# Pairs of channels parted by ScalarE ahead of the matmuls, in a matmul with a decayed cumulative sum

## The chip, the cores and the metric

The kernel runs on one core of a Trainium2 chip. The metric is device time in microseconds (us); three runs of the kernel before gave 987.27, 988.52 and 989.05 us, median 988.52. The engines are PE (TensorE, with its weight loads listed as PEld), DVE (VectorE), ACT (ScalarE), POOL (GpSimd) and SP (SyncE, which here only issues DMAs). Each works through its own queue in order.

## The reference

```python
B, S, D = 16, 2048, 1024                      # x is B x S x D, w is D x D, decay is D
xw = x @ w
out[:, 0, :] = xw[:, 0, :]
for t in range(1, S):
    out[:, t, :] = decay[None, :] * out[:, t - 1, :] + xw[:, t, :]
```

A matmul over channels, and then along time, for each batch and output channel, a first-order recurrence. Everything is float32 outside; the matmul runs in bf16.

## The kernel before

**Chunks and groups.** Time is cut into 64 chunks of 512 steps (four to a batch). A group is one or two chunks; the output of a group is made in eight tiles n = 0 to 7 of 128 output channels, T = 512 or 1024 time steps wide. The groups are [0], [1], then pairs [2, 3] to [60, 61], then [62] and [63] (L126). The word slot is used for one tile's turn in the order of the program, and step for its number over the whole run in the changed kernel.

**Input.** `load(c, q)` (L107) is a DMA from POOL's queue that brings a quarter of the channels of chunk c, turned to bf16 on the way, into 32 partitions of a buffer `xb` (four buffers). `turn(c)` (L117) transposes a whole chunk on DVE in blocks of 32 x 32. It treats two neighbouring bf16 channels as one float32, so that one transpose of 2048 float32 does for the chunk; in the result `xt` the two channels of a pair lie side by side at every time step, `[128, M, TL, 2]`. The matmul for channel block k reads `xt[:, k // 2, :, k % 2]`, every second bf16 (L136).

**Matmul.** Each tile takes eight matmuls of 128 x 128 by 128 x 512 per chunk (k = 0 to 7), accumulated in PSUM. Three PSUM buffers of T = 1024 rotate. In the first group the first six tiles are computed with k outermost, while the weights still arrive (`heads`, L277 on). 4096 matmuls in all.

**The recurrence.** A plain tile is scanned by DVE straight out of PSUM over all T steps (L193), which also frees the PSUM buffer. A tile whose n is in `PAIRED` (five of the eight) goes another way. `pair()` (L168): ACT copies the tile out of PSUM into `xs` (L172) and makes decay times the even steps (L162); POOL adds that to the odd steps (L178). `scan()`: DVE scans only the odd steps, with decay squared (`dec2`), T/2 long (L184). `complete()`: ACT multiplies the odd results by decay (L162 again) and POOL adds the even inputs (L206); ACT also keeps the last step for the next group (L209). `back()` (L211) transposes a finished tile on DVE into the output buffer `ot` (two buffers, which also hold the raw weights at the start). After tile 7 of a group `store` sends `ot` out in four DMAs, one per quarter of the partitions, on SP's queue. The last group has no pairwise tiles, and stores in two halves.

**What sets the order.** `pin` keeps instructions in the order of the program on their engines. `behind(new)` writes that order: `pair` of the new tile, the scan of the tile before it if pairwise, the scan of the new tile if plain, `complete` of the tile before, and then `back`: of a pairwise tile two slots after its matmuls, of a plain one a slot after. `feed(step, after)` (L243) follows each tile: at n = 1 and n = 4 it turns the chunks of the next group and appends the loads that their buffers then allow; then it issues one load, or two if more than four wait.

**The start.** Loads of chunk 0, 16 loads of the weights, eight weight copies (DVE and ACT in turn, L98 and L100) and four tiny loads of decay on ACT's queue behind ACT's copies; then the loads of chunks 1 to 3 and, on DVE, the product `dec2` (L85) and `turn(0)`.

Of the kernel before, what the change touches and what calls it, by code (L numbers as in the profile page):

```python
# [9 lines left out]
FP32 = mybir.dt.float32  # L10
BF16 = mybir.dt.bfloat16
ALU = mybir.AluOpType


def _ap(ap_obj: bass.AP, new_ap, extra_offset=0):
    return dataclasses.replace(
        ap_obj,
        ap=[list(p) for p in new_ap],
        offset=ap_obj.offset + extra_offset,
    )  # L20
# [5 lines left out]
def kernel(  # L26
# [17 lines left out]

    nc = tc.nc
    pin = tc.keep_in_program_order
    B, S, D = x.shape  # L50
# [2 lines left out]
    NQ = 4  # L53
    P = 32
    CQ = D // NQ
    K = CQ // P
    M = K // 2
    TL = 512
    NJ = TL // P
    NC = S // TL  # L60
    PAIRED = (0, 1, 3, 4, 6)
    TURNS = (1, 4)

    const = ctx.enter_context(tc.tile_pool(name="const", bufs=1))
    xbp = ctx.enter_context(tc.tile_pool(name="xbp", bufs=4))
    xtp = ctx.enter_context(tc.tile_pool(name="xtp", bufs=4))
    sop = ctx.enter_context(tc.tile_pool(name="sop", bufs=4))
    tmp = ctx.enter_context(tc.tile_pool(name="tmp", bufs=2))
    otp = ctx.enter_context(tc.tile_pool(name="otp", bufs=2))
    psp = ctx.enter_context(tc.tile_pool(name="psp", bufs=3, space=bass.MemoryType.PSUM))  # L70
    pdp = ctx.enter_context(tc.tile_pool(name="pdp", bufs=1, space=bass.MemoryType.PSUM))

    def quad(q):
        return slice(q * P, (q + 1) * P)

    dec = const.tile([128, K], FP32, name="dec")
    dec2 = pdp.tile([128, 512], FP32, name="dec2")
    wsb = const.tile([128, K, K, NQ, P], BF16, name="wsb")

    def load_dec():  # L80
        with nc.allow_non_contiguous_dma(reason="a vector of 1024"):
            for q in range(NQ):
                pin(nc.scalar.dma_start(
                    out=dec[quad(q), :], in_=_ap(decay, [[1, P], [P, K]], q * CQ)))
        pin(nc.vector.tensor_tensor(out=dec2[:, 0:K], in0=dec, in1=dec, op=ALU.mult))  # L85

    def load_w():
        wb = otp.tile([128, M, 2 * D], BF16, name="ot")
        for m in range(M):
            for q in range(NQ):  # L90
                pin(nc.gpsimd.dma_start(  # L91
                    out=wb[quad(q), m],
                    in_=_ap(w, [[2 * D, P], [1, 2 * D]], (q * CQ + m * 2 * P) * D)))
        for k in range(K):
            dst = wsb[:, k].rearrange("p n q i -> p q n i")
            src = wb.rearrange("p m (e q n i) -> p (m e) q n i", e=2, q=NQ, n=K)[:, k]
            if k % 2:
                pin(nc.scalar.copy(out=dst, in_=src))  # L98
            else:
                pin(nc.vector.tensor_copy(out=dst, in_=src))  # L100

    chunks = [(b, c * TL) for b in range(B) for c in range(NC)]
    nch = len(chunks)
    xt_of = {}
    xb_of = {}

    def load(c, q):  # L107
        if c >= nch:
            return
        b, t0 = chunks[c]  # L110
        if q == 0:
            xb_of[c] = xbp.tile([128, NJ, CQ], BF16, name="xb")
        pin(nc.gpsimd.dma_start(  # L113
            out=xb_of[c][quad(q)],
            in_=_ap(x, [[D, P], [P * D, NJ], [1, CQ]], (b * S + t0) * D + q * CQ)))

    def turn(c):  # L117
        xt = xtp.tile([128, M, TL, 2], BF16, name="xt")
        src = xb_of.pop(c).rearrange("p j c -> p (j c)").bitcast(FP32)
        dst = xt.rearrange("p m t e -> p (m t e)").bitcast(FP32)  # L120
        pin(nc.vector.transpose(  # L121
            out=dst.rearrange("p (m j i) -> p j m i", m=M, i=P),
            in_=src.rearrange("p (j m c) -> p j m c", m=M, c=P)))
        xt_of[c] = xt

    groups = [[0], [1]] + [[c, c + 1] for c in range(2, nch - 2, 2)] + [[nch - 2], [nch - 1]]  # L126
    for g in groups:
        assert chunks[g[0]][0] == chunks[g[-1]][0]

# [2 lines left out]
    def matmul(ps, n, k, xt):  # L132
        pin(nc.tensor.matmul(  # L133
            out=ps,
            lhsT=wsb[:, k, n].rearrange("p q i -> p (q i)"),
            rhs=xt[:, k // 2, :, k % 2],  # L136
            start=(k == 0),
            stop=(k == K - 1),
        ))

    class Tile:
# [3 lines left out]
        def __init__(self, gi, n, ps, ot):  # L145
            g = groups[gi]
            self.b, self.t0 = chunks[g[0]]
            self.T = TL * len(g)
            self.n, self.ps, self.ot = n, ps, ot
            self.final = gi + 1 == len(groups)  # L150
            self.paired = n in PAIRED and not self.final
            self.so = sop.tile([128, self.T + 2], FP32, name="so")
            self.prev = None if self.t0 == 0 else last[n]
            if self.t0 + self.T < S:
                last[n] = const.tile([128, 1], FP32, name=f"keep{n}", bufs=2)
                self.keep = last[n]
            else:
                self.keep = None
# [52 lines left out]
        def back(self):  # L211
            T, n = self.T, self.n
            pin(nc.vector.transpose(  # L213
                out=self.ot[:, :, n * P:(n + 1) * P],
                in_=self.so[:, 2:T + 2].rearrange("p (i t) -> p i t", t=P)))
            if self.final:
                if n == K // 2 - 1:
                    self.store(0, K // 2)
                elif n == K - 1:
                    self.store(K // 2, K)  # L220
            elif n == K - 1:
                self.store(0, K)
# [8 lines left out]

    for q in range(NQ):
        load(0, q)
    load_w()
    load_dec()
    for c in range(1, 4):
        for q in range(NQ):
            load(c, q)
    turn(0)
    loads = [(4, q) for q in range(NQ)]  # L240
    next_load = 5

    def feed(step, after):  # L243

        nonlocal next_load
        for at, c in zip(TURNS, after):
            if step == at:
                turn(c)
                loads.extend((next_load, q) for q in range(NQ))
                next_load += 1  # L250
        for _ in range(2 if len(loads) > NQ else 1):
            if loads:
                load(*loads.pop(0))
# [3 lines left out]
    def behind(new):  # L257

        if new is not None:
            new.pair()  # L260
        before = waiting[-1] if waiting else None
        if before is not None and before.paired:
            before.scan()
        if new is not None and not new.paired:
            new.scan()
        if before is not None:
            before.complete()
        waiting.append(new)
        if len(waiting) == 4:
            waiting.pop(0)  # L270
        for tl, lag in ((waiting[0] if len(waiting) == 3 else None, True),
                        (before, False)):
            if tl is not None and tl.paired == lag:
                tl.back()

    for gi, g in enumerate(groups):
        T = TL * len(g)  # L277
        ot = otp.tile([128, T // P, CQ], FP32, name="ot")
        xts = [xt_of.pop(c) for c in g]
        after = groups[gi + 1] if gi + 1 < len(groups) else []  # L280
        if gi == 0:
            heads = [psp.tile([128, 2, TL], FP32, name="ps") for _ in range(3)]
            for k in range(K):
                for n in range(6):
                    matmul(heads[n // 2][:, n % 2], n, k, xts[0])
        for n in range(K):
            if gi == 0 and n < 6:
                ps = heads[n // 2][:, n % 2]
            else:
                ps = psp.tile([128, T], FP32, name="ps")  # L290
                for k in range(K):
                    for l in range(len(g)):
                        matmul(ps[:, l * TL:(l + 1) * TL], n, k, xts[l])
            behind(Tile(gi, n, ps, ot))
            feed(n, after)
    behind(None)
    behind(None)

# [29 lines left out]
```

## Time and profile before

| | |
|---|---|
| runs, us | 987.27, 988.52, 989.05 |
| profiled execution, us | 987.84 |
| its span, us | 986.1 |
| mean granted clock of TensorE | 0.992 |
| traffic with HBM | 138.42 MB read, 134.22 MB written |

The span runs from the first to the last instruction; the execution's time has 1.7 us more around it. A group of instructions is named by its line, engine, operation and the tiles it writes and reads; a row by form also keeps shapes apart, and gives busy us, mean ns of one, and the idle time ahead of it with what ended it. In a row of the windows view stand the stretch, its length, the busy time of each engine with the number of instructions, the granted clock, the DMA share and GB/s. A row of the timeline gives the start, the duration, the engine, the operation, the count, and in brackets the idle time before and what ended it.

### The profile page before, as it was taken

The page shows a single profiled execution, that of the slowest core. Times are in us where ns is not written, and L with a number is a line of the kernel's source. Part 1 is how long each engine was busy: PE and PEld are TensorE (multiplying, and loading weights), DVE is VectorE, ACT ScalarE, POOL GpSimd, SP SyncE. Part 2 cuts the span into 40 slices and gives each one's busy share as a digit, 9 for nine tenths or more (in the row PEclk, how much of TensorE's full clock was granted, in tenths as well). Part 3 has the DMA queues.
Part 4 walks back from the last instruction along what each step waited for, and adds up shares of the span by engine and source line. Part 5 has one row for each costly group of instructions (what it writes and reads, how often), then busy time and mean ns, then how long its engine had stood idle before and what let it go on. Part 6 is the DMA issues. An engine that isn't in the chain of part 4 may idle for free.

```text
span 986.1 us, 11189 instructions
## 1 busy us (share of the span) xinstructions
PE 926.9 (94%) x4015; PEld 392.6 (40%) x4096; DVE 853.3 (87%) x613; ACT 393.3 (40%) x729; POOL 581.8 (59%) x686
## 2 busy tenths in 40 slices
PE   0589999999999999999999999999999999999994
PEld 0234444444444444444444444444444444444441
DVE  0299999898999989899998999999899899999894
ACT  2154444434444443444444344444444434444440
POOL 6276666566656656665666666566666666564440
PEclk9999999999999999999999999999999999999997
DMA  9899999999999999999999999999999999997757
GB/s 161 106 182 195 177 219 218 220 220 225 215 214 219 213 223 224 222 216 214 217 217 221 223 221 211 217 215 219 221 227 219 212 215 218 219 222 174 170 138 205
DMA packets 272440, 204.18 MB, mean 207 GB/s; under 512 B 7680, under 2 KB 271872, under 8 KB 272384
## 3 DMA queue, kind: packets, MB, share of 16 engines
q1 hardware_dynamic: 133248, 133.18, 54.2%
q0 software_dynamic: 135936, 69.22, 51.8%
q10 hardware_dynamic: 3200, 1.05, 0.5%
q8 instruction: 32, 0.52, 0.2%
q14 instruction: 24, 0.20, 0.0%
HBM read 138.42 MB, written 134.22 MB: 276 GB/s over the span
## 4 chain that ended last, share of the span: by engine, by line
PE 88%; issue 4%; DMA 3%; DVE 2%; POOL 2%; SPq 0%; ACT 0%; DVEq 0%; POOLq 0%
PE ps L133 88%; DMA out_dram<-ot 2%; DMA xb<-in_x_dram 2%; DVE so L193 1%; POOL xb L113 1%; DVE ot L213 1%; POOL ot L91 0%; POOL xs L178 0%; SPq L227 0%; DVE so L184 0%; DVE xt L121 0%; ACT h L162 0%; ACT xs L172 0%; POOL so L206 0%; DVEq L323 0%
## 5 line engine op out<-in xcount | busy, mean ns | idle before, releaser
L133 PE MATMUL ps<-xt,wsb 128*128 128x512 bf16 x4015 | 926.9, 389 | 49.9 <-DVE xt L121 31.6
L133 PEld LDWEIGHTS <-wsb 128*128 128x128 bf16 x4096 | 392.6, 96 | 583.7 <-issue 37.7
L178 POOL TENSOR_TENSOR xs<-h,xs 128x512 f32<-128x512 f32 (+1 forms) x165 | 206.3, 1250 | 293.4 <-ACT so L177 101.9
L213 DVE STREAM_TRANSPOSE ot<-so 128x1024 f32<-128x1024 f32 (+1 forms) x272 | 300.0, 1150 | 7.8 <-DMA out_dram<-ot 6.2
L172 ACT COPY xs<-ps 128x1024 f32<-128x1024 f32 (+1 forms) x165 | 160.6, 973 | 324.0 <-PE ps L133 285.7
L206 POOL TENSOR_TENSOR so<-h,xs 128x512 f32<-128x512 f32 (+1 forms) x165 | 206.2, 1250 | 71.7 <-ACT keep L209 37.5
L162 ACT ACTIVATE h<-so,dec 128x512 f32<-128x512 f32 (+1 forms) x165 | 122.0, 740 | 222.6 <-DVE so L184 222.6
L113 POOL DMA_DIRECT2D xb<-in_x_dram x256 | 169.1, 662 | 5.2 <-DMA xb<-in_x_dram 2.8
L121 DVE STREAM_TRANSPOSE xt<-xb 128x2048 f32<-128x2048 f32 x64 | 146.3, 2286 | 0.0
L184 DVE TENSOR_TENSOR_SCAN so<-dec,xs 128x512 f32<-128x512 f32 (+1 forms) x80 | 95.3, 1191 | 56.4 <-POOL xs L178 35.8
L184 DVE TENSOR_TENSOR_SCAN so<-dec,keep,xs 128x512 f32<-128x512 f32 (+1 forms) x85 | 103.5, 1218 | 34.1 <-POOL xs L178 32.3
L193 DVE TENSOR_TENSOR_SCAN so<-dec,keep,ps 128x1024 f32<-128x1024 f32 (+1 forms) x59 | 122.0, 2069 | 0.5 <-PE ps L133 0.5
L162 ACT ACTIVATE h<-ps,dec 128x512 f32<-128x512 f32 (+1 forms) x165 | 111.2, 674 | 0.0
L193 DVE TENSOR_TENSOR_SCAN so<-dec,ps 128x1024 f32<-128x1024 f32 (+1 forms) x48 | 105.3, 2194 | 0.0
L209 ACT COPY keep<-so 128x1 f32<-128x1 f32 x144 | 26.7, 185 | 0.6 <-DVE so L193 0.5
L100 DVE COPY wsb<-ot 128x1024 bf16<-128x1024 bf16 x4 | 1.8, 449 | 19.8 <-DMA ot<-in_w_dram 19.8
L177 ACT COPY so<-keep 128x1 f32<-128x1 f32 x85 | 16.3, 192 | 0.0
L91 POOL DMA_DIRECT2D ot<-in_w_dram x16 | 7.8, 493 | 4.9 <-DMA xb<-in_x_dram 3.8
L175 POOL MEMSET so<- 128x1 f32 x80 | 9.0, 112 | 0.0
L98 ACT ACT_TABLE_LOAD x1 | 1.3, 1283 | 13.6 <-DMA ot<-in_w_dram 13.6
L85 DVE TENSOR_TENSOR dec<-dec 128x8 f32<-128x8 f32 x1 | 0.2, 175 | 7.5 <-DMA dec<-in_decay_dram 7.5
L98 ACT COPY wsb<-ot 128x1024 bf16<-128x1024 bf16 x4 | 4.2, 1045 | 3.1 <-DMA ot<-in_w_dram 3.1
(4 smaller groups left out, 0.4 us busy)
## 6 DMA issues: line engine op xcount, KB each, us to landing
out_dram<-ot SPq DMA_DIRECT2D x120, 1024.0 KB, 14.8
xb<-in_x_dram POOLq DMA_DIRECT2D x256, 256.0 KB, 9.2
out_dram<-ot SPq DMA_DIRECT2D x12, 512.0 KB, 9.3
ot<-in_w_dram POOLq DMA_DIRECT2D x16, 128.0 KB, 4.8
out_dram<-ot SPq DMA_DIRECT2D x4, 256.0 KB, 4.0
out_dram<-ot ACTq DMA_DIRECT2D x4, 256.0 KB, 4.4
dec<-in_decay_dram ACTq DMA_DIRECT2D x4, 1.0 KB, 6.0
```

The source lines that it names most:

```text
L113: pin(nc.gpsimd.dma_start(out=xb_of[c][quad(q)], in_=_ap(x, [[D, P], [P * D, NJ], [1, CQ]], (b * S + t0) * D + q * CQ)))
L121: pin(nc.vector.transpose(out=dst.rearrange("p (m j i) -> p j m i", m=M, i=P), in_=src.rearrange("p (j m c) -> p j m c", m=M, c=P)))
L133: pin(nc.tensor.matmul(out=ps, lhsT=wsb[:, k, n].rearrange("p q i -> p (q i)"), rhs=xt[:, k // 2, :, k % 2], start=(k == 0), stop=(k == K ...
L162: pin(nc.scalar.activation(out=h, in_=src, func=mybir.ActivationFunctionType.Copy, scale=dec[:, self.n:self.n + 1]))
L172: pin(nc.scalar.copy(out=self.xs, in_=self.ps))
L177: pin(nc.scalar.copy(out=self.so[:, 1:2], in_=self.prev))
L178: pin(nc.gpsimd.tensor_tensor(out=self.xs[:, 1:T:2], in0=g, in1=self.xs[:, 1:T:2], op=ALU.add))
L184: pin(nc.vector.tensor_tensor_scan(out=so[:, 3:T + 2:2], data0=dec2[:, n:n + 1].to_broadcast([128, T // 2]), data1=self.xs[:, 1:T:2], init ...
L193: pin(nc.vector.tensor_tensor_scan(out=so[:, 2:T + 2], data0=dec[:, n:n + 1].to_broadcast([128, T]), data1=self.ps, initial=0.0 if self.pr ...
L206: pin(nc.gpsimd.tensor_tensor(out=so[:, 2:T + 2:2], in0=h, in1=self.xs[:, 0:T:2], op=ALU.add))
L209: pin(nc.scalar.copy(out=self.keep, in_=so[:, T + 1:T + 2]))
L213: pin(nc.vector.transpose(out=self.ot[:, :, n * P:(n + 1) * P], in_=self.so[:, 2:T + 2].rearrange("p (i t) -> p i t", t=P)))
```

## The change

- The transposed pairs land in a new tile `xw` (two buffers). `part(c, copy, m0, m1)` copies half of a chunk from `xw` into `xt`, now `[128, M, 2, TL]`, so that the even and odd channels of a pair lie apart and each matmul reads consecutive bf16. In the steady state both halves are ACT copies; for chunks 0 and 1 one half is DVE's.
- `PAIRED` is (0, 1, 2, 4, 5, 6) instead of (0, 1, 3, 4, 6).
- A fixed agenda takes the place of `TURNS`: for each chunk, counted back from the first step of its group, turn, first part and second part stand 11, 10 and 8 steps ahead (first chunk of two) or 7, 6 and 4 steps ahead (second chunk, or a chunk by itself). Each turn appends the loads of chunk c + 3; there are three `xb` buffers instead of four, and five `xt` instead of four.
- The groups are [0], [1, 2], [3], [4, 5] to [60, 61], [62], [63]. Chunks 0 and 3 share one `ot` buffer, a half each, and so do 62 and 63. Tiles of one chunk share a PSUM buffer two by two. The last three groups store in two halves.
- At the start the decay loads go out on SP's queue first; only chunks 1 and 2 are loaded ahead; `dec2`, `turn(0)` and its parts precede the weight copies on DVE and ACT (two of eight on ACT); `turn(1)` and its parts follow them, ahead of the first tile.

```diff
-    PAIRED = (0, 1, 3, 4, 6)
-    TURNS = (1, 4)
+    PAIRED = (0, 1, 2, 4, 5, 6)
...
-    xbp = ctx.enter_context(tc.tile_pool(name="xbp", bufs=4))
-    xtp = ctx.enter_context(tc.tile_pool(name="xtp", bufs=4))
+    xbp = ctx.enter_context(tc.tile_pool(name="xbp", bufs=3))
+    xwp = ctx.enter_context(tc.tile_pool(name="xwp", bufs=2))
+    xtp = ctx.enter_context(tc.tile_pool(name="xtp", bufs=5))
...
+    def part(c, copy, m0, m1):
+        if m0 == 0:
+            xt_of[c] = xtp.tile([128, M, 2, TL], BF16, name="xt")
+        pin(copy(
+            out=xt_of[c][:, m0:m1],
+            in_=xw_of[c][:, m0:m1].rearrange("p m t e -> p m e t")))
+
+    groups = ([[0], [1, 2], [3]] + [[c, c + 1] for c in range(4, nch - 2, 2)]
+              + [[nch - 2], [nch - 1]])
...
-            rhs=xt[:, k // 2, :, k % 2],
+            rhs=xt[:, k // 2, k % 2],
...
+            self.halved = gi + 3 >= len(groups)
...
-            if self.final:
+            if self.halved:
...
-    load_w()
-    load_dec()
-    for c in range(1, 4):
+    wv = load_w()
+    for c in range(1, 3):
         for q in range(NQ):
             load(c, q)
+    pin(nc.vector.tensor_tensor(out=dec2[:, 0:K], in0=dec, in1=dec, op=ALU.mult))
     turn(0)
...
+    part(0, nc.vector.tensor_copy, 0, 2)
+    part(0, nc.scalar.copy, 2, M)
+    for k in range(K):
+        copy = nc.scalar.copy if k % 4 == 3 else nc.vector.tensor_copy
+        pin(copy(out=wsb[:, k].rearrange("p n q i -> p q n i"), in_=wv[:, k]))
+    loads = []
+    agenda = {}
+
+    def prepare(c, l, first):
+        def turned():
+            turn(c)
+            loads.extend((c + 3, q) for q in range(NQ))
+        ahead = (7, 6, 4) if l else (11, 10, 8)
+        steps = (turned, lambda: part(c, nc.scalar.copy, 0, 2),
+                 lambda: part(c, nc.scalar.copy, 2, M))
+        for a, f in zip(ahead, steps):
+            agenda.setdefault(first - a, []).append(f)
+
+    for gi, g in enumerate(groups):
+        for l, c in enumerate(g):
+            if c > 1:
+                prepare(c, l if len(g) == 2 else 1, gi * K)
+    loads.extend((3, q) for q in range(NQ))
+    turn(1)
+    loads.extend((4, q) for q in range(NQ))
+    part(1, nc.vector.tensor_copy, 0, 2)
+    part(1, nc.scalar.copy, 2, M)
...
-        ot = otp.tile([128, T // P, CQ], FP32, name="ot")
+        if len(g) == 2:
+            ot = otp.tile([128, T // P, CQ], FP32, name="ot")
+        else:
+            if g[0] in (0, nch - 2):
+                halves = otp.tile([128, 2 * TL // P, CQ], FP32, name="ot")
+            ot = halves[:, g[0] % 2 * NJ:(g[0] % 2 + 1) * NJ]
```

More of the change, by code (lines that the diff above doesn't have):

```diff
@@ L78 @@
     wsb = const.tile([128, K, K, NQ, P], BF16, name="wsb")
[L80 to L85, printed above, removed]
+    with nc.allow_non_contiguous_dma(reason="a vector of 1024"):
+        for q in range(NQ):
+            nc.sync.dma_start(
+                out=dec[quad(q), :], in_=_ap(decay, [[1, P], [P, K]], q * CQ))
     def load_w():
@@ L93, in load_w @@
                     in_=_ap(w, [[2 * D, P], [1, 2 * D]], (q * CQ + m * 2 * P) * D)))
[L94 to L100, printed above, removed]
+        return wb.rearrange("p m (e q n i) -> p (m e) q n i", e=2, q=NQ, n=K)
     chunks = [(b, c * TL) for b in range(B) for c in range(NC)]
@@ L104 @@
     xt_of = {}
+    xw_of = {}
     xb_of = {}
@@ L117, in turn @@
     def turn(c):
-        xt = xtp.tile([128, M, TL, 2], BF16, name="xt")
+        xw = xwp.tile([128, M, TL, 2], BF16, name="xw")
         src = xb_of.pop(c).rearrange("p j c -> p (j c)").bitcast(FP32)
-        dst = xt.rearrange("p m t e -> p (m t e)").bitcast(FP32)
+        dst = xw.rearrange("p m t e -> p (m t e)").bitcast(FP32)
         pin(nc.vector.transpose(
@@ L123, in turn @@
             in_=src.rearrange("p (j m c) -> p j m c", m=M, c=P)))
-        xt_of[c] = xt
-    groups = [[0], [1]] + [[c, c + 1] for c in range(2, nch - 2, 2)] + [[nch - 2], [nch - 1]]
+        xw_of[c] = xw
+    def part(c, copy, m0, m1):
[6 more added lines that the diff above has]
+              + [[nch - 2], [nch - 1]])
     for g in groups:
@@ L233, with feed @@
         load(0, q)
-    load_w()
-    load_dec()
-    for c in range(1, 4):
+    wv = load_w()
+    for c in range(1, 3):
         for q in range(NQ):
             load(c, q)
+    pin(nc.vector.tensor_tensor(out=dec2[:, 0:K], in0=dec, in1=dec, op=ALU.mult))
     turn(0)
[L240 to L250, printed above, removed]
+    part(0, nc.vector.tensor_copy, 0, 2)
[23 more added lines that the diff above has]
+    part(1, nc.scalar.copy, 2, M)
+    def feed(step):
+        for f in agenda.pop(step, []):
+            f()
         for _ in range(2 if len(loads) > NQ else 1):
@@ L277 @@
         T = TL * len(g)
-        ot = otp.tile([128, T // P, CQ], FP32, name="ot")
+        if len(g) == 2:
[4 more added lines that the diff above has]
+            ot = halves[:, g[0] % 2 * NJ:(g[0] % 2 + 1) * NJ]
         xts = [xt_of.pop(c) for c in g]
-        after = groups[gi + 1] if gi + 1 < len(groups) else []
         if gi == 0:
@@ L286 @@
         for n in range(K):
-            if gi == 0 and n < 6:
-                ps = heads[n // 2][:, n % 2]
-            else:
-                ps = psp.tile([128, T], FP32, name="ps")
+            if len(g) == 2:
+                ps = psp.tile([128, T], FP32, name="ps")
+            else:
+                if gi == 0 and n < 6:
+                    both = heads[n // 2]
+                elif n % 2 == 0:
+                    both = psp.tile([128, 2, TL], FP32, name="ps")
+                ps = both[:, n % 2]
+            if gi > 0 or n >= 6:
                 for k in range(K):
@@ L294 @@
             behind(Tile(gi, n, ps, ot))
-            feed(n, after)
+            feed(gi * K + n)
     behind(None)
```

## The prediction

> **What bounds the kernel now.** I read the page's busy and chain lines first, then one whole steady group in the windows view (a group is two chunks, 128 matmuls).
>
> ```profile
> PE 926.9 (94%) x4015; PEld 392.6 (40%) x4096; DVE 853.3 (87%) x613; ACT 393.3 (40%) x729; POOL 581.8 (59%) x686
> PE 88%; issue 4%; DMA 3%; DVE 2%; POOL 2%; SPq 0%; ACT 0%; DVEq 0%; POOLq 0%
> 500.00:528.90 28.90, 28.71 (x126) 12.22 (x128) 26.51 (x19) 12.13 (x22) 18.23 (x23) 1.00 1.13 218
> ```
>
> The chain is PE for 88%. In the group (length, then PE, weight loads, DVE, ACT, POOL, granted clock, DMA share, GB/s) PE is busy for all but 0.2 of 28.90 us, at full clock, so its rate is 28.90/128 = 225.8 ns a matmul; the 128 weight loads count the matmuls, two of whose records are missing. DVE is at 92% (26.51), ACT 42%, POOL 63%. A faster matmul pays until DVE's work no longer fits.
>
> Is 225.8 ns the rate of the array itself? The weight-load timeline late in the run, at granted clock 0.50, tells it: one load per matmul.
>
> ```profile
> 969.03 0.14 PEld L133 LDWEIGHTS <-wsb 128*128 128x128 bf16 x1 [0.28 <-issue]
> ...
> 973.29 0.14 PEld L133 LDWEIGHTS <-wsb 128*128 128x128 bf16 x1 [0.28 <-issue]
> ```
>
> Eleven loads, ten steps: 4.26/10 = 426 ns at half clock, so 213 ns for the same columns at full clock. Full clock shows 225.8: some 12.5 ns a matmul do not shrink with the clock. They are either in how the moving operand is read (every second bf16, the `k % 2` of a pair) or in something the change leaves alone, such as the change of weights.
>
> **The change, part by part.** The durations, by form:
>
> ```profile
> L213 DVE STREAM_TRANSPOSE ot<-so 128x1024 f32<-128x1024 f32 x240 | 279.5, 1212 | 0.9 <-POOL so L206 0.3
> L178 POOL TENSOR_TENSOR xs<-h,xs 128x512 f32<-128x512 f32 x150 | 195.1, 1301 | 272.3 <-ACT so L177 100.8 <-ACT h L162 84.8 <-ACT keep L209 49.7
> L172 ACT COPY xs<-ps 128x1024 f32<-128x1024 f32 x150 | 151.8, 1012 | 299.5 <-PE ps L133 261.8 <-POOL so L175 27.7 <-remote 10.1
> L121 DVE STREAM_TRANSPOSE xt<-xb 128x2048 f32<-128x2048 f32 x64 | 146.3, 2286 | 0.0
> L162 ACT ACTIVATE h<-so,dec 128x512 f32<-128x512 f32 x150 | 114.2, 761 | 202.5 <-DVE so L184 202.5
> L193 DVE TENSOR_TENSOR_SCAN so<-dec,keep,ps 128x1024 f32<-128x1024 f32 x45 | 104.5, 2322 | 0.0
> L162 ACT ACTIVATE h<-ps,dec 128x512 f32<-128x512 f32 x150 | 104.0, 693 | 0.0
> L184 DVE TENSOR_TENSOR_SCAN so<-dec,keep,xs 128x512 f32<-128x512 f32 x75 | 96.3, 1285 | 33.6 <-POOL xs L178 31.8
> L172 ACT COPY xs<-ps 128x512 f32<-128x512 f32 x15 | 8.8, 584 | 24.5 <-PE ps L133 23.9 <-DVE so L193 0.5
> L162 ACT ACTIVATE h<-ps,dec 128x256 f32<-128x256 f32 x15 | 7.2, 481 | 0.0
> L98 ACT COPY wsb<-ot 128x1024 bf16<-128x1024 bf16 x4 | 4.2, 1045 | 3.1 <-DMA ot<-in_w_dram 3.1
> L100 DVE COPY wsb<-ot 128x1024 bf16<-128x1024 bf16 x4 | 1.8, 449 | 19.8 <-DMA ot<-in_w_dram 19.8
> ```
>
> *Unit-stride matmuls.* 4096 matmuls; the new spacing lies between 213 (all of the 12.5 ns goes) and 225.8 (none). The half-clock rows are the nearest measure of a matmul that waits for nothing, so I go near them and leave a fifth of the excess as a start cost: 216 ns. A group is then 27.65 us, and the sum gets 4096 x 9.8 ns = **-40.1 us** (ends -52 and 0). The Trainium skill, "TensorE: Matmul & The Clock Gate", section "Wait — 56ns, not 53.3ns?", gives 426.7 ns cold and 215.7 ns warm start to start at N = 512; the cold figure agrees with the 426 above, the warm one is 10 ns under the 225.8, and by it this term would be -41.4.
>
> *The parting copies.* Two copies of 128x2048 bf16 a chunk, four a group, on ACT. Nearest row: 1045 ns for 1024 bf16. Two of them are 2.09; the f32 row pair (584 for 512, 1012 for 1024) gives 0.84 ns an element, so 1.87; four times the 761 of the strided 512-element read gives 3.04. I take 2.0. ACT per group: 12.13 + one more pair set, at most 1.01 + 0.69 + 0.76 = 2.5, + 8.0 = 22.6 of 27.65; at 3.04 it is 26.8. It fits. In ACT's queue a part stands ahead of the next tile's copy out of PSUM. It falls in slots 0, 2, 4, 6: in 0 and 4 ACT has about 1.9 + 0.2 + 2.0 = 4.1 us for a slot of 3.46, so tiles 1 and 5 are read some 0.6 us late; slots 3 and 7, without a pair, take up the rest. PE asks for that PSUM buffer again two slots (6.9 us) after the tile's end, so this costs **0**.
>
> *Six of eight pairwise.* DVE loses a 2.32 scan and gains a 1.29 one: 26.51 - 1.03 = 25.5 of 27.65, the same 92%. POOL gains two adds: 18.23 + 2.6 = 20.8. What hides both is the PE's group; if DVE lost its 2.1 us of slack, each further microsecond would cost some 29 us in all. **0**.
>
> *The start.* The timeline and the chain's DMA pieces:
>
> ```profile
> 29.13 0.17 DVE L85 TENSOR_TENSOR dec<-dec 128x8 f32<-128x8 f32 x1 [7.51 <-DMA dec<-in_decay_dram]
> 29.22 2.31 DVE L121 STREAM_TRANSPOSE xt<-xb 128x2048 f32<-128x2048 f32 x1
> 31.58 12.82 PE L133 MATMUL ps<-xt,wsb 128*128 128x512 bf16 x48 [31.58 <-DVE xt L121]
> 45.39 1.97 PE L133 MATMUL ps<-xt,wsb 128*128 128x512 bf16 x7 [1.00 <-ACT h L162]
> 50.96 1.97 PE L133 MATMUL ps<-xt,wsb 128*128 128x512 bf16 x8 [3.60 <-ACT h L162]
> 55.50 34.80 PE L133 MATMUL ps<-xt,wsb 128*128 128x512 bf16 x142 [2.57 <-DVE so L193]
> ```
> ```profile
> 3.36 7.63 DMA xb<-in_x_dram
> 18.83 7.66 DMA xb<-in_x_dram
> ```
> ```profile
> xb<-in_x_dram POOLq DMA_DIRECT2D x256, 256.0 KB, 9.2
> out_dram<-ot SPq DMA_DIRECT2D x12, 512.0 KB, 9.3
> ...
> dec<-in_decay_dram ACTq DMA_DIRECT2D x4, 1.0 KB, 6.0
> ```
>
> Chunk 0 has landed by 10.99, yet its transpose runs at 29.22: DVE's queue holds the weight copies and then dec2, which waits for the four decay loads behind ACT's copies. The change puts those loads on the idle SP queue first (they may delay chunk 0 by about 1 us, an estimate: a part of the 6.0 us that they take to land) and the transpose before the weights: 11.0 + 1.0 + 2.3 + 1.1 (half a part on DVE: 2 x 0.449, up to 2.3 if it runs like the transpose) + 0.45 (first weight copy) = first matmul at 16, 15.6 earlier. Then the three idle times, 1.00 + 3.60 + 2.57 = 7.2, get a successor. Before's first 48 matmuls took 12.82 where 48 x 0.2258 = 10.84 were due, so some nine ran at half rate; 48 x 0.216 and nine times 0.21 more end at 28.3. But ACT's queue now has part(1) ahead of pair(0): chunk 1 lands at 26.49 (second DMA piece), turn to 28.8, part to 30.8, two short pairs of 0.584 + 0.481 to 32.9. PE idles 4.6. n = 6, 7 end near 38; the next group needs chunk 2's second half, which stands on ACT behind two more pairs (2.1), the first part (2.0) and waits for DVE's scans and the turn, some 4, and takes 2.0 itself: near 43, another 3.4 us or so. 8.0 against 7.2: the start is worth **-15** (-17 to -8).
>
> *The loads.* Four moved loads (chunk 3) go from POOL's start queue to behind its first adds; they land some 9.2 us after issue, and their transpose is at step 9, after 45 us. Three xb buffers instead of four leave loads 41 us of lead at one turn per 13.8. **0**.
>
> *A new wait.* Chunk 3 as a group of its own stores from the half of an `ot` buffer whose next user is the very next group, [4, 5]. Rows: one batch of SP stores, and all stores' landing; the 512 KB row stands above.
>
> ```profile
> 510.99 9.53 SPq L227 DMA_DIRECT2D out_dram<-ot  x4
> DMA to landing us min/median/max: 3.3/12.0/21.2
> ```
>
> [1, 2] ends near 70 (38 + 3.4 + 27.65 and its waits) and issues its 4 MB at 75.9 (scan 7 and three transposes later: 2.3 + 3 x 1.2), which holds SP 9.5 us; by the longest landing, 21.2, the last is in at 97. [3] ends at 84; its 512 KB stores stand behind and need about 9.3 more: 106. back(0) of [4, 5] is reached on DVE's in-order queue at 84 + 3 x 3.46 and a scan, 95.7. Behind it wait scans 2 and 3, ACT's complete(2) for scan 2, and ACT's pair(4). PE fills three PSUM buffers, to 84 + 6 x 3.46 = 104.7, and restarts once DVE has done back(0), scan 2 and scan 3 (1.2 + 1.3 + 2.3): 110.8, 6.1 later, and a few matmuls at half clock: **+6.5** (0 if the stores land six us sooner, 13 if as much later).
>
> *The end.*
>
> ```profile
> 966.72 0.71 DVE L213 STREAM_TRANSPOSE ot<-so 128x512 f32<-128x512 f32 x1 [6.22 <-DMA out_dram<-ot]
> 968.64 8.15 PE L133 MATMUL ps<-xt,wsb 128*128 128x512 bf16 x24 [4.85 <-DVE so L193]
> 976.83 1.28 DVE L193 TENSOR_TENSOR_SCAN so<-dec,keep,ps 128x512 f32<-128x512 f32 x1
> ```
>
> The last group waits for [60, 61]'s store; the two last chunks sharing one buffer removes this: 4.85 idle, and 8.15 - 24 x 0.2258 = 2.7 at half clock. Late next: DVE, which no longer rests there and reaches its last scan some 2.5 us further behind PE, and ACT with two parts in the short group 62 (about 0.6). **-4.5** (-8 to +2).
>
> **Sum.** 986.1 - 40.1 - 15 + 6.5 - 4.5 = 933.0 of span. The profiled execution took 987.84, 1.7 over its span, and the median of the runs is 0.7 above that: **935 us**. With the bounds of the terms this case lies in 918 to 952.
>
> **Rivals.** *The spacing stays.* The 12.5 ns belong to the weight change, and unit stride buys nothing; then 935 + 40 = **975**. For it: weights change before every matmul (x4096 loads). The Trainium skill has a rule on this side: "Advanced Engine Details and Errata", section "SBUF Cachelines", asks for two hits on a 16-byte line for full rate, and a stride of two bf16 still has four; by it the copies would be bought for nothing. Against it: a load lasts 0.14 us at half clock and 0.096 (392.6/4096) on average and lies beside the matmul in both. Chance 0.12.
>
> *DMA becomes the bound.*
>
> ```profile
> DMA packets 8380, 6.30 MB, mean 218 GB/s; under 512 B 192, under 2 KB 8378, under 8 KB 8378
> DMA packets 2889, 2.19 MB, mean 243 GB/s; under 512 B 54, under 2 KB 2888, under 8 KB 2888
> ```
>
> The first row is the steady group, whose DMA share above is 1.13. Were 220 GB/s the ceiling, 6.30 MB would take 28.6 us, 0.95 over the new group, for some 29 groups: **963**. Against it is the second row, nine of those microseconds (524 to 533) with loads and stores mixed: 243 GB/s, 25.9 us a group. Chance 0.07.
>
> *ACT becomes the bound, and the kernel is slower.* Without the matmul's gain the sum stands at 975. Slower than before takes a group of 29.4 us, so 14.6 + 4p = 29.4: a part p of 3.7 us or more in every slot 0, 2, 4, 6. At 4.2 the group is 31.4 and the run 975 + 29 x 2.5 = **1047**. For it: no row has a bf16 read at a stride on ACT. Against it: all three bounds above are under 3.1. Chance 0.05.
>
> **Numbers.** Forecast 0.73, stays 0.12, DMA 0.07, ACT 0.05, and 0.03 for smaller in-order stalls between. The range 918 to 966 holds nearly all of the forecast, the DMA case and the stalls, 0.80. Faster by over 0.2% (2 us, about what these runs can tell from no change; they spread by 1.8) are all but the ACT case and a sliver: 0.94; within 0.01; slower 0.05.
>
> **What would show it.** Right: 128 weight loads in 27.65 us instead of 28.90; parts near 2.0 us on ACT; first matmul near 16; one long DVE wait for `out_dram<-ot` near 95 us with PE idle some 6 us soon after, none near 960; DVE at 92%. Wrong: still 28.9; PE waiting on ACT's copies in every group; turns waiting for `xb` loads; the [4, 5] wait absent or above 15 us.

## The result, and the profile after

The changed kernel takes 959.83 us (median of four runs, 959.45 to 961.64) against 988.34 for the kernel before: ratio 0.9716, 95% interval 0.9699 to 0.9733. The time lies in the predicted range of 918 to 966, 25 us above the predicted 935 and above the 952 that the forecast's own case reached to. The profiled execution has a span of 957.6 us.

The page's busy and chain lines of the changed kernel:

```profile
PE 891.8 (93%) x4096; PEld 401.9 (42%) x4096; DVE 828.7 (87%) x617; ACT 687.5 (72%) x969; POOL 662.5 (69%) x768
PE 88%; POOL 3%; issue 2%; DVE 2%; DMA 1%; ACT 1%; DVEq 0%; ACTq 0%; POOLq 0%
```

PE is still 88% of the chain; ACT went from 40% to 72%. A steady group in the windows view, and the part copies by form:

```profile
500.00:527.63 27.63, 27.63 (x130) 12.54 (x128) 25.33 (x19) 21.58 (x30) 20.31 (x24) 1.00 1.15 220
```
```profile
L121 ACT COPY xt<-xw 128x2048 bf16<-128x2048 bf16 x126 | 239.7, 1902 | 19.3 <-DVE xw L113 19.3
L113 DVE STREAM_TRANSPOSE xw<-xb 128x2048 f32<-128x2048 f32 x64 | 146.3, 2286 | 9.9 <-DMA xb<-in_x_dram 9.9
```

128 weight loads now fit in 27.63 us instead of 28.90: 215.9 ns a matmul. DVE has 25.33 of it, ACT 21.58, and no engine makes PE wait here. What came out otherwise is at the two ends. PE's own timeline, every stretch with the idle time before it:

```profile
15.47 12.13 PE L133 MATMUL ps<-xt,wsb 128*128 128x512 bf16 x48 [15.47 <-DVE wsb L245]
33.69 3.57 PE L133 MATMUL ps<-xt,wsb 128*128 128x512 bf16 x8 [6.09 <-ACT h L163]
45.35 33.26 PE L133 MATMUL ps<-xt,wsb 128*128 128x512 bf16 x144 [8.09 <-ACT h L163]
79.71 3.61 PE L133 MATMUL ps<-xt,wsb 128*128 128x512 bf16 x16 [1.11 <-ACT h L163]
85.64 3.61 PE L133 MATMUL ps<-xt,wsb 128*128 128x512 bf16 x16 [2.32 <-ACT h L163]
90.70 3.61 PE L133 MATMUL ps<-xt,wsb 128*128 128x512 bf16 x16 [1.44 <-ACT h L163]
95.41 804.78 PE L133 MATMUL ps<-xt,wsb 128*128 128x512 bf16 x3728 [1.10 <-ACT h L163]
901.25 3.61 PE L133 MATMUL ps<-xt,wsb 128*128 128x512 bf16 x16 [1.05 <-ACT h L163]
907.09 3.61 PE L133 MATMUL ps<-xt,wsb 128*128 128x512 bf16 x16 [2.22 <-ACT h L163]
912.23 3.61 PE L133 MATMUL ps<-xt,wsb 128*128 128x512 bf16 x16 [1.53 <-ACT h L163]
916.94 3.61 PE L133 MATMUL ps<-xt,wsb 128*128 128x512 bf16 x16 [1.10 <-ACT h L163]
922.04 3.61 PE L133 MATMUL ps<-xt,wsb 128*128 128x512 bf16 x16 [1.48 <-DVE so L194]
927.12 3.61 PE L133 MATMUL ps<-xt,wsb 128*128 128x512 bf16 x16 [1.47 <-DVE so L194]
932.21 3.61 PE L133 MATMUL ps<-xt,wsb 128*128 128x512 bf16 x16 [1.48 <-DVE so L194]
937.23 1.89 PE L133 MATMUL ps<-xt,wsb 128*128 128x512 bf16 x8 [1.41 <-DVE so L194]
```

The middle runs 3728 matmuls without a gap. The gaps are all in groups of one chunk, [0], [3], [62] and [63], and nearly always after 16 matmuls, which is two tiles. From these rows and the rows of before the whole difference can be added up. The first matmul comes 31.58 - 15.47 = 16.1 us sooner. From first to last matmul before took 976.79 - 31.58 = 945.2, of which 4096 x 0.2258 = 924.9 are matmuls and 20.3 are lost; after, 939.12 - 15.47 = 923.7, 884.2 and 39.5. Behind the last matmul stand 9.3 us before (986.1 - 976.8) and 18.5 after (957.6 - 939.1). So: -16.1 - 40.7 + 19.2 + 9.2 = -28.4, and the spans differ by 28.5. Two new losses of 19 and 9 us eat half of what the matmuls and the start gained.

For the second of them, SP's waits, and at the end of the run ACT's stores of group 63, SP's last twelve stores and DVE's last transposes:

```profile
SPq L228 <- DMA out_dram<-ot: 32.2, 4, 25.2
```
```profile
932.79 9.74 ACTq L228 DMA_DIRECT2D out_dram<-ot  x4
935.90 17.23 SPq L228 DMA_DIRECT2D out_dram<-ot  x12
...
940.35 1.28 DVE L214 STREAM_TRANSPOSE ot<-so 128x512 f32<-128x512 f32 x2
```

SP waits 25.2 us at one stretch for a store to land: its last twelve stores, the eight of group 62 among them, go out only from 935.9 on. The last output is finished at 941.6, yet the span ends at 957.6.

### The profile page after: what moved, and what is told of

It is laid out like the page before. It is cut to its first block, busy times and chain, and to the rows that moved or that the text cites. A ratio compares the mean times of both kernels' runs of the same rounds, so it can differ in the third digit from the quotient of the medians.

```text
span 957.6 us, 11691 instructions
## 1 busy us (share of the span) xinstructions
PE 891.8 (93%) x4096; PEld 401.9 (42%) x4096; DVE 828.7 (87%) x617; ACT 687.5 (72%) x969; POOL 662.5 (69%) x768
## 4 chain that ended last, share of the span: by engine, by line
PE 88%; POOL 3%; issue 2%; DVE 2%; DMA 1%; ACT 1%; DVEq 0%; ACTq 0%; POOLq 0%
PE ps L133 88%; POOL xb L105 1%; DMA xb<-in_x_dram 1%; DVE so L194 1%; DVE ot L214 1%; POOL ot L88 1%; POOL xs L179 0%; ACT xs L173 0%; DVE so L185 0%; ACT h L163 0%; POOL so L207 0%; DVE xw L113 0%; ACT xt L121 0%; DVEq L355 0%; POOL so L176 0%
## 5 line engine op out<-in xcount | busy, mean ns | idle before, releaser
L133 PE MATMUL ps<-xt,wsb 128*128 128x512 bf16 x4096 | 891.8, 381 | 47.4 <-ACT h L163 26.1
L179 POOL TENSOR_TENSOR xs<-h,xs 128x512 f32<-128x512 f32 (+1 forms) x198 | 246.6, 1246 | 221.4 <-ACT h L163 100.8
L173 ACT COPY xs<-ps 128x1024 f32<-128x1024 f32 (+1 forms) x198 | 193.1, 975 | 179.6 <-PE ps L133 178.0
L207 POOL TENSOR_TENSOR so<-h,xs 128x512 f32<-128x512 f32 (+1 forms) x198 | 245.4, 1240 | 29.0 <-ACT h L163 16.1
L121 ACT COPY xt<-xw 128x2048 bf16<-128x2048 bf16 x126 | 239.7, 1902 | 19.3 <-DVE xw L113 19.3
L163 ACT ACTIVATE h<-so,dec 128x512 f32<-128x512 f32 (+1 forms) x198 | 148.9, 752 | 27.0 <-DVE so L185 23.2
L113 DVE STREAM_TRANSPOSE xw<-xb 128x2048 f32<-128x2048 f32 x64 | 146.3, 2286 | 9.9 <-DMA xb<-in_x_dram 9.9
L163 ACT ACTIVATE h<-ps,dec 128x512 f32<-128x512 f32 (+1 forms) x198 | 133.2, 673 | 0.0
L194 DVE TENSOR_TENSOR_SCAN so<-dec,keep,ps 128x1024 f32<-128x1024 f32 (+1 forms) x42 | 84.8, 2019 | 5.4 <-PE ps L133 4.6
L194 DVE TENSOR_TENSOR_SCAN so<-dec,ps 128x1024 f32<-128x1024 f32 (+1 forms) x32 | 70.2, 2194 | 1.7 <-PE ps L133 1.7
```

Source lines behind the costliest of these rows:

```text
L113: pin(nc.vector.transpose(out=dst.rearrange("p (m j i) -> p j m i", m=M, i=P), in_=src.rearrange("p (j m c) -> p j m c", m=M, c=P)))
L121: pin(copy(out=xt_of[c][:, m0:m1], in_=xw_of[c][:, m0:m1].rearrange("p m t e -> p m e t")))
L133: pin(nc.tensor.matmul(out=ps, lhsT=wsb[:, k, n].rearrange("p q i -> p (q i)"), rhs=xt[:, k // 2, k % 2], start=(k == 0), stop=(k == K - 1),))
L163: pin(nc.scalar.activation(out=h, in_=src, func=mybir.ActivationFunctionType.Copy, scale=dec[:, self.n:self.n + 1]))
L173: pin(nc.scalar.copy(out=self.xs, in_=self.ps))
L179: pin(nc.gpsimd.tensor_tensor(out=self.xs[:, 1:T:2], in0=g, in1=self.xs[:, 1:T:2], op=ALU.add))
```

## The experiments

Two theories for the missing 25 us. The first: the tiles of a one-chunk group that share a PSUM buffer wait for each other. The second: the stores at the end are held by something other than their data. Rivals: ACT simply has too much to do in a short group, and the DMA engines cannot store faster at the end. A third question is whether the gain itself comes from the stride.

**All stores on SP's queue.**

```diff
-                queue = nc.scalar if self.final and q >= 2 else nc.sync
+                queue = nc.sync
```

> All stores of the last group go through SP's queue, none through ACT's; nothing else changes. Theory: the stores of group 62 are held for 25 us by a semaphore shared with a store of group 63 on ACT's queue, and so everything is sent after 935.8; with one queue they go out as soon as their transposes are done, and the end comes some 5 us after the last transpose (941.6): 8 to 11 us less than the changed kernel. Rival: the end is set by the DMA engines, which have 8 MB to store in the last 60 us, and the order of issue hardly counts: 0 to 3 us less.

951.96 us (951.04 to 952.30), 7.9 under the changed kernel, just short of the 8 to 11 expected; ratio to before 0.9632 (0.9617 to 0.9646). SP's waits near the end, and PE's last stretch:

```profile
SPq L228 <- DVE ot L214: 46.0, 7, 16.9
SPq L355 <- DMA out_dram<-ot: 2.5, 3, 1.1
```
```profile
938.86 1.89 PE L133 MATMUL ps<-xt,wsb 128*128 128x512 bf16 x8 [1.41 <-DVE so L194]
```

SP now waits only for DVE's transposes, and for landings in its very last instructions. Behind the last matmul stand 950.4 - 940.75 = 9.7 us instead of 18.5. So the stores of group 62 were held, not slow. In the built program of the changed kernel the first of them waits for a semaphore that the store of group 63 on ACT's queue uses just ahead of it, and the first store of group 62's second half waits in the same way for an ACT store that itself waits for the last transposes: stores do not stand under `pin`, and their semaphores had been given out in another order than the data become ready.

**A PSUM buffer for each tile of a one-chunk group.**

```diff
-                    both = heads[n // 2]
-                elif n % 2 == 0:
-                    both = psp.tile([128, 2, TL], FP32, name="ps")
-                ps = both[:, n % 2]
+                    ps = heads[n // 2][:, n % 2]
+                else:
+                    ps = psp.tile([128, T], FP32, name="ps")
```

> Each tile of a one-chunk group (beyond the first six of the first group) gets a PSUM buffer of its own again, as in the kernel before. Theory: PE waits in these groups because the odd tile's matmuls wait until ACT has read the even tile from the shared buffer; PE's idle time before n = 7 of the first group (8.1 us), in group 3 (6.0) and in groups 62 and 63 (11.7) falls to 10 us or less in all, and the run by 10 to 18 us. Rival: ACT has more work in a short group (some 18 us with its parts) than PE (13.8), and PE waits for it whatever buffer the tile has: the idle time stays above 20 us, the run falls by 0 to 5 us.

947.42 us (946.22 to 948.67), 12.4 less; ratio to before 0.9587 (0.9571 to 0.9604). The idle time in front of n = 7 in the first group is 3.0 instead of 8.1, that in group 3 falls from 6.0 to 2.5, that in groups 62 and 63 from 11.7 to 3.6. The first two of these, by PE's rows:

```profile
40.00 42.70 PE L133 MATMUL ps<-xt,wsb 128*128 128x512 bf16 x184 [3.01 <-DVE so L194]
85.22 816.99 PE L133 MATMUL ps<-xt,wsb 128*128 128x512 bf16 x3776 [2.53 <-DVE so L194]
```

The theory's numbers hold, although ACT has the same work in these groups as in the changed kernel.

**Both tiles computed before either is read.**

```diff
                 elif n % 2 == 0:
                     both = psp.tile([128, 2, TL], FP32, name="ps")
+                    for e in range(2):
+                        for k in range(K):
+                            matmul(both[:, e], n + e, k, xts[0])
                 ps = both[:, n % 2]
-            if gi > 0 or n >= 6:
+            if len(g) == 2:
```

> The shared PSUM buffers stay, but in one-chunk groups the matmuls of both tiles of a buffer are issued ahead of the first reading of either. Theory of the shared buffer: PE no longer waits between the two; ACT and DVE get the even tile 1.7 us later instead; PE's idle time in these groups falls from 26 to about 10 us, the run by 8 to 16 us. Rival (ACT's work in short groups): 0 to 5 us.

946.22 us (945.99 to 946.63), 13.6 less; ratio to before 0.9574 (0.9558 to 0.959). PE from the end of the steady part:

```profile
106.33 795.29 PE L133 MATMUL ps<-xt,wsb 128*128 128x512 bf16 x3684 [0.84 <-DVE so L194]
902.70 13.11 PE L133 MATMUL ps<-xt,wsb 128*128 128x512 bf16 x60 [1.08 <-ACT xt L121]
```

The buffers are shared as before, and only the order of two tiles' matmuls and their readers differs. The last two groups now have one gap of 1.08 us instead of eight, and the last matmul ends at 915.8 instead of 939.1. The wait was thus an ordering: a matmul that writes one half of the buffer stood behind the readers of the other half. In the built program of the changed kernel the first matmul of tile 7 does wait for the instruction by which ACT reads tile 6, from the other half: the program's dependencies keep the two halves as one thing. The same halves as two separate tiles were not tried. Of the 23 us that PE gained only 14 reached the end, because the stores were still held: 28.9 us of the span lie behind the last matmul.

**The stride by itself.**

```diff
-            xt_of[c] = xtp.tile([128, M, 2, TL], BF16, name="xt")
+            xt_of[c] = xtp.tile([128, M, TL, 2], BF16, name="xt")
...
-            in_=xw_of[c][:, m0:m1].rearrange("p m t e -> p m e t")))
+            in_=xw_of[c][:, m0:m1]))
...
-            rhs=xt[:, k // 2, k % 2],
+            rhs=xt[:, k // 2, :, k % 2],
```

> ACT's and DVE's part copies copy straight, without parting the channel pairs, and the matmul reads every second bf16 again; every copy, wait and buffer else is as in the changed kernel. Theory: the stride of the moving operand costs 10 ns a matmul, so spacing is 225.8 ns, the group 28.9 us, and the run 959.8 + 38 to 41 = 998 to 1001 us, slower than the kernel before. Rival: the 10 ns went with another edit (buffers, the engines' load on SBUF): spacing stays 216 and the run near 960.

999.62 us (999.31 to 999.91), ratio to before 1.0115 (1.01 to 1.013): slower than before, and 39.8 above the changed kernel. The steady group:

```profile
500.00:528.90 28.90, 28.90 (x129) 12.22 (x128) 25.60 (x19) 21.39 (x28) 20.97 (x26) 1.00 1.11 215
```

128 weight loads in 28.90 us again. The long stretch of 3728 matmuls, which took 804.78 us in the changed kernel, says it more finely:

```profile
97.58 842.07 PE L133 MATMUL ps<-xt,wsb 128*128 128x512 bf16 x3728 [1.10 <-ACT h L163]
```

That is 225.9 ns a matmul against 215.9. With every copy and every wait in place the stride alone costs 10 ns a matmul. Everything else in the change together, the copies, the start and the new waits, is worth +11 us. The parting itself is free on ACT: its copies take 1904 ns straight and 1902 ns parted. On DVE they take 694 and 1226.

The prediction's half-clock reading can now be made with consecutive elements too. The changed kernel's weight loads at granted clock 0.50:

```profile
45.73 0.15 PEld L133 LDWEIGHTS <-wsb 128*128 128x128 bf16 x1 [0.27 <-issue]
...
49.14 0.15 PEld L133 LDWEIGHTS <-wsb 128*128 128x128 bf16 x1 [0.28 <-issue]
```

Nine loads, eight steps: 426 ns, as with the stride. So at half clock the stride costs nothing, and of the 12.8 ns between 213 and 225.8 the stride is 9.9. The other 2.9 stay with consecutive elements.

**The two remedies together.** With a buffer for each tile:

> Both edits together: all stores on SP's queue, and a PSUM buffer of its own for each tile of a one-chunk group. Theory: the two losses are separate, the held stores after the last transpose and PE's waits ahead of it; together they give about the sum of what they gave alone (7.9 and 12.4): 937 to 941 us. Rival: the DMA engines cannot take the stores faster once they start earlier: 944 us or more.

937.27 us (936.76 to 937.91), ratio 0.9488 (0.9473 to 0.9502); and with two tiles first:

> All stores on SP's queue, and both tiles of a shared PSUM buffer computed before either is read. With the second edit alone the last transpose ends at 923.7 and the span at 944.7. Theory: without the held stores the last ones land some 5 us after the last transpose, span near 930, run 930 to 934 us. Rival (DMA engines): 938 us or more.

932.56 us (932.05 to 932.83), ratio 0.9439 (0.9425 to 0.9453). The second is the better one; 27.3 us under the changed kernel, more than 7.9 + 13.6, since the held stores had hidden part of PE's gain. DVE's last transposes:

```profile
922.47 1.27 DVE L214 STREAM_TRANSPOSE ot<-so 128x512 f32<-128x512 f32 x2
```

They end at 923.7 and the span at 931.0, 7.3 us later. With SP's queue alone the last transposes ended at 943.3 and the span at 950.4, 7.1 later: with PE done 25 us earlier the last stores still follow as closely, and the DMA rival falls.

**Five of eight pairwise.**

```diff
-    PAIRED = (0, 1, 2, 4, 5, 6)
+    PAIRED = (0, 1, 3, 4, 6)
```

> As the kernel with both edits (SP stores, two tiles first), but with tiles 0, 1, 3, 4, 6 pairwise as before, five of eight. The prediction's account of DVE (26.5 of a 27.65 us group by the rows of before): still fits, PE gets no new idle time between 110 and 880 us, 0 to 3 us more than its twin. Rival: at 96% DVE, with its waits for POOL, becomes the bound; the group takes 0.5 to 1.5 us more, the run 14 to 43 us more.

935.39 us (935.28 to 935.64), 2.8 over its twin, ratio to before 0.9469 (0.9453 to 0.9484). The steady 600 us, first of the twin with six, then with five:

```profile
200.00:800.00 600.00, 600.00 (x2782) 272.05 (x2780) 554.69 (x392) 468.34 (x632) 445.34 (x500) 1.00 1.16 228
```
```profile
200.00:800.00 600.00, 600.00 (x2782) 272.00 (x2781) 567.98 (x392) 418.96 (x557) 392.58 (x448) 1.00 1.15 228
```

DVE goes from 92.4% to 94.7% and PE does not notice: 600.00 busy in both. The long stretch of PE, with six and with five, which ends 60 matmuls before the last in both:

```profile
106.39 795.29 PE L133 MATMUL ps<-xt,wsb 128*128 128x512 bf16 x3684 [1.56 <-DVE so L194]
```
```profile
95.88 809.10 PE L133 MATMUL ps<-xt,wsb 128*128 128x512 bf16 x3748 [1.48 <-DVE so L194]
```

Both run at 215.9 ns a matmul, but the one with five ends at 905.0 instead of 901.7. Six of eight thus gains its 3 us in the first groups, ahead of this stretch; behind it five of eight is 0.7 us shorter.

**The new start alone, in the kernel before.**

```diff
-    load_w()
-    load_dec()
+    wb = load_w()
...
+    pin(nc.vector.tensor_tensor(out=dec2[:, 0:K], in0=dec, in1=dec, op=ALU.mult))
     turn(0)
+    copy_w(wb)
```

(and the decay loads ahead of all others, on SP's queue)

> The kernel before with one part of the change: the decay loads go first, on SP's queue, and the product and the first chunk's transpose stand ahead of the weight copies. Theory (the prediction's step on the start): first matmul near 14.5 us instead of 31.6; as ACT has no parts to make here, the next waits do not grow, and 13 to 17 us are gained: 971 to 975 us. Rival: the chunks that follow arrive no sooner, PE waits for their loads, and less than 6 us are gained.

970.83 us (970.26 to 972.18), ratio to before 0.9829 (0.9814 to 0.9844), 17.1 us less.

```profile
14.35 13.46 PE L135 MATMUL ps<-xt,wsb 128*128 128x512 bf16 x48 [14.35 <-DVE wsb L102]
28.81 1.97 PE L135 MATMUL ps<-xt,wsb 128*128 128x512 bf16 x8 [1.00 <-ACT h L164]
35.04 3.57 PE L135 MATMUL ps<-xt,wsb 128*128 128x512 bf16 x8 [4.27 <-ACT h L164]
```

The first matmul is 17.2 us sooner, and the waits that follow (1.00, 4.27, 0.96, 0.27) are 6.5 in all, no more than the 7.2 of before: the whole step reaches the end, a hair more than expected.

**Chunk 1's second part on DVE**, in the kernel of 932.56 us.

```diff
-    part(1, nc.scalar.copy, 2, M)
+    part(1, nc.vector.tensor_copy, 2, M)
```

> The kernel with SP stores and two tiles first (932.6 us), and chunk 1's second part made by DVE, so that ACT's queue has no part ahead of the first tiles' copies. Theory: the 5.5 us in which PE waits for ACT after the first 48 matmuls come from that part standing in ACT's queue; the wait shrinks to 1 to 3 us. But the two parts of chunk 2 on ACT are late next, so that of the 3 to 4 us freed only 1 to 3 reach the end: 929.5 to 931.5 us. Rival: the wait is for something else (the PSUM buffer's other reader, the loads), and stays above 5 us.

932.09 us (931.11 to 932.51), ratio to before 0.9434 (0.9421 to 0.9447); the twin, on another chip, has 0.9439 (0.9425 to 0.9453), so no difference can be told. PE's start, in the twin and then in this kernel:

```profile
33.11 5.03 PE L133 MATMUL ps<-xt,wsb 128*128 128x512 bf16 x16 [5.55 <-ACT h L163]
39.69 2.10 PE L133 MATMUL ps<-xt,wsb 128*128 128x512 bf16 x9 [1.54 <-DVE so L194]
```
```profile
28.97 3.61 PE L133 MATMUL ps<-xt,wsb 128*128 128x512 bf16 x15 [1.04 <-ACT h L163]
39.05 50.79 PE L133 MATMUL ps<-xt,wsb 128*128 128x512 bf16 x220 [6.47 <-DVE so L194]
```

The wait was the part in ACT's queue: without it 1.04 is left of 5.55. But all of it comes back one tile pair later, as 6.47 instead of 1.54. There PE waits for DVE's scan of tile 3, in the twin and then in this kernel:

```profile
38.44 1.19 DVE L194 TENSOR_TENSOR_SCAN so<-dec,ps 128x512 f32<-128x512 f32 x1
```
```profile
37.81 1.19 DVE L194 TENSOR_TENSOR_SCAN so<-dec,ps 128x512 f32<-128x512 f32 x1
```

DVE gets to it only 0.6 us sooner, because it begins its first scan at the same time in both (33.06 and 33.07) and turns chunk 2 before the next. Fewer microseconds than the expected 1 to 3 came through.

## Why the prediction was right, and where it was not

*The matmul.* -40.1 was predicted, the stride measures 39.8. Reading the half-clock rows beside the full-clock ones gave the size of the excess, and 216 ns came out as 215.9. The mechanism was right; that a fifth of the excess would stay was assumed without a row behind it, and there the forecast was also lucky. The Trainium skill, "TensorE: Matmul & The Clock Gate", section "Wait — 56ns, not 53.3ns?", has 215.7, and the trace agrees.

*The parts, and six of eight.* 1.90 us a part against 2.0, ACT 21.58 against 22.6, DVE 25.33 against 25.5, and no wait of PE in the steady part, as predicted. The ACT rival falls with the first number. The DMA rival falls too: windows of the changed kernel move 220 GB/s and more, and in the kernel of 932.56 us 228, without PE waiting.

*The start.* First matmul at 15.47 against 16. Of the two waits behind it the first was priced (4.6; 6.09 came), for the reason given. The second was put at 3.4, as a wait for chunk 2; it was 8.09, and it was tile 7 waiting for ACT to read tile 6. With the start order alone -17.1 was measured. In the changed kernel the first matmul's 16.1 less 7.0 of longer waits leave -9.1, so the -15 was 6 too much, most of it by the shared buffer.

*The shared buffer.* This is the step that failed. The prediction said that PE asks for a PSUM buffer again two slots after a tile's end, and put ACT's lateness at 0. That holds for groups of two chunks. In groups of one the change puts two tiles in one buffer, and PE asks for it at once. The edit stood in the diff and was given no term. The gaps there are 8.09 in the first group, 5.97 in the third, 11.74 in the last two: 25.8 us, against which the prediction had 3.4 and 0.6. The two PSUM experiments remove 16.7 and 21.6 of them, in two different ways; what is left cannot be put down to the shared buffer alone.

*The new wait on `ot`.* +6.5 was predicted; it came to 0.55. DVE's row and SP's in the changed kernel:

```profile
109.08 1.25 DVE L214 STREAM_TRANSPOSE ot<-so 128x1024 f32<-128x1024 f32 x1 [0.55 <-DMA out_dram<-ot]
```
```profile
83.52 25.21 SPq L228 DMA_DIRECT2D out_dram<-ot  x8
```

SP was still issuing group 3's last store at 108.7, and DVE went on at 109.08: it did not wait for those stores. In the built program [4, 5] has the address of [1, 2]'s buffer, not that of the shared one. The step took the two buffers to alternate. The pool seems to give out the one that is released first; only this one address speaks for it. That this wait stayed away happened to cancel the gaps in group 3, which were not foreseen either.

*The end.* -4.5 was predicted. The gap of 4.85 before the last group is gone, as said; in its place stand 11.7 us of gaps, of which a buffer for each tile takes away 8.1, and the held stores, which the experiment with SP's queue puts at 8 us. Both were missed. The rough sum of the misses, 6 at the start, 12 in PE's gaps at the end and 7 behind the last matmul, is the 25 us by which 935 was too low. With both mended the time is 932.6, but that it lies so near to 935 is in part chance: the forecast held 6.5 us for a wait on `ot` that never came. The result lies in the stated range of 918 to 966 only by luck: it is outside the 918 to 952 given for the forecast's own case, and the part above 952 was held for the DMA rival and the stalls. The 918 to 952 does not follow from the terms as given either: their low ends together give 911, their high ends 995.

## What to carry to other kernels

Compare the spacing of matmuls at the lower granted clock with that at full clock: what does not scale may be a cost that can be removed. Here 9.9 of 12.8 ns were the stride of the moving operand, and the rest stayed; only the run with nothing but the stride changed could tell them apart. For every buffer that a change makes two tiles share, ask separately in each kind of group who reads it and how soon the next writer comes. And where transfers of one output go through two queues, look at what each issue waits for: a semaphore taken in another order can hold finished data.

## What the runs showed of the hardware that was not expected

A moving operand of 128x512 bf16 that takes every second element costs 225.8 ns a matmul at full clock and 215.9 with consecutive elements, while at half clock both show 426 ns, just the double of 213. The Trainium skill, "Advanced Engine Details and Errata", section "SBUF Cachelines", asks for two hits on a 16-byte line for full performance; this stride has four, and still pays 10 ns, so the measurement speaks against reading the rule that way. Why four hits do not hide it at full clock, the runs do not show. On ACT the same stride of reading costs nothing in a copy of 128x2048 bf16 (1902 ns against 1904), while on DVE it takes 1226 ns against 694.
